# One core, a streaming encoder step: finer norm stages, other kept weights and row buffers; factors begun a tile earlier, kept down weights, a last group of four

## The chip, the cores and the metric

The kernel runs on one core of a Trainium2 chip. The metric is the device time of one execution in microseconds. The kernel before takes 2319.67 us (median of three runs, 2317.66 to 2321.96).

## What is computed

One inference step of an encoder with one layer, in float32, for 2048 prompt rows and 32 sample rows of width 1024:

```python
h = layer_norm(x, ln_in_g, ln_in_b)
z = h @ w_in                                  # 2304 columns: three head groups
o = concat(rg_lru(...), retention(...), sliding_window_attention(...))
h = layer_norm(ALPHA * h + o @ w_out, ln1_g, ln1_b)
f = (silu(h @ w_gate) * (h @ w_up)) @ w_down  # 2816 inner columns
h = layer_norm(ALPHA * h + f, ln2_g, ln2_b)
```

The states of the three groups (convolution rows, recurrent state, retention state, keys and values) are outputs too.

## The kernel before, in words

Each float32 product is made of three products in the fast 32-bit form: an operand is split into a high part (a copy on ScalarE, ACT) and a low part (a subtraction on VectorE, DVE), and high x high, low x high and high x low are added up in PSUM. So each weight tile that TensorE (PE) uses costs a load (issued by SyncE, SP), a copy on ACT (L250 or L1401) and a subtraction on DVE (L254 or L1406), unless the split pair is stored in memory once and loaded back whole.

**First half.** The rows go through six blocks of 256 to 384 rows. For each block there are 18 `W` units (input projection, L908), the three mixers (`mix_a`, `mix_b`, `mix_c`) and 8 `O` units (output projection, L995 to L997), then a layer norm (`ln1`), and the normed rows go to memory twice: as rows, and transposed as columns (`to_memory`: PE transposes into an `sd` bank, ACT copies to one of three `stg` buffers, ACT's queue stores it). Block 0 goes through its gate, up and down products (`G` and `D` units) at the end of this half; `columns0` loads its columns back, `accumulate` (L1024, L1026) adds the down products to the rows. `feed` sets the order of weight loads on SP: up to three staged raw tiles, or a pair kept in memory by an earlier block. `keeps` and `known` say which block stores a pair and which blocks load it: units with odd x are stored by block 1, those with even x by block 2. The side work (norms, mixers, transposes) is written as generators; before each unit `step` lets them go on, one yield at a time, as long as a credit of DVE time lasts. `pipeline` runs the tiles of one stage together; with `apart` set it hands over after each tile's piece. This decides in which order DVE and ACT see the pieces.

**Second half.** The other 1792 rows form two parts of 896. Gate and up products go by f, 22 tiles of 128 inner columns, in `gu`: seven products of 12 matmuls (L1578) with seven left factors (`a11`, `s1`, `s2`, `a12`, `a22`, `s3`, `s4`; sums and differences of quarter matrices, split, made by `columns_first` and `columns_rest` for part 0 and by `columns` for part 1) and seven right factors (`b11`, `t1` and so on, from the weights). Down products go by groups of f in `down` (L1646 to L1648, for 7 row tiles x 2 halves x each f), whose bank `d_add` (L1653) adds to the rows; `GROUPSS` sets the groups, `due` when each comes. Weights are jobs in one list, done ahead in the order of that list by `background` as far as six raw tiles (`ww`) and seven pairs allow. Pairs of the sums `t1` to `t4` are stored in part 0 (`w_keep`) and loaded in part 1 (`w_known`); those of the down weights are made anew in both parts. `ln2` norms finished rows as side work. The last group of part 1 is done in `finale`: five banks are begun with all but the last f, then tile by tile the rest, `stats` (L1711, L1713) and `scales` (L1716, L1717, the power on GpSimd (POOL), L1718) on the tile, and `centre` (L1721), `normal` (ACT, L1726) and `affine` (DVE L1733, POOL L1734) one tile behind.

Row tiles (`tok`) are one pool of 11; PSUM has four `mm` banks, four `sd` banks in the first half, and four `gu` banks from `change()` on, which is called at f = 14 of block 0.

Of the kernel before, what the change touches and what calls it, by code (L numbers as in the profile page):

```python
# [41 lines left out]
GROUPSS = (((0, 3), (3, 6), (6, 9), (9, 12), (12, 15), (15, 17), (17, 19), (19, 22)),) * 2  # L42
# [55 lines left out]
def tile_hybrid_step(ctx: ExitStack, tc: tile.TileContext, io, outs):  # L98
# [190 lines left out]
    def step():  # L289
# [67 lines left out]
    def norm(name, b, g, be):  # L357
# [27 lines left out]
        yield from pipeline([tile_(t, rows) for t, (_, rows) in enumerate(ttiles(b))], 1)  # L385
# [37 lines left out]
    def to_memory(b):  # L423

        def half(t, c0, rows, h):
# [4 lines left out]
            stg = sb.tile([128, 4, 128], F32, name="stg", bufs=3)  # L430
# [33 lines left out]
    def columns0():  # L464
# [3 lines left out]
        for k0, k1 in ((0, 3), (3, 6), (6, 8)):  # L468
            w = row_tile()[:, :(k1 - k0) * n].rearrange("p (k c) -> p k c", c=n)
            sp.dma_start(w, cols0[:, k0:k1, :])  # L470
            yield from wait(4)
# [193 lines left out]
    def mix_b(b):  # L665
# [11 lines left out]
        def chunk(c0, n, state, gi):  # L677
# [56 lines left out]
            yield 0.0  # L734
            pt = sdbank().rearrange("p (f c) -> p f c", f=4)
# [533 lines left out]
    def columns_first():  # L1269

        a = [two(), two()]
# [37 lines left out]

    def columns(s):  # L1310

        for n in ("a11", "s1", "s2", "a12", "a22", "s3", "s4"):
            factor(n)
        ws = []
        for i in range(2):
            k, w = slice(2 * i, 2 * i + 2), {}
            for x, th, kh in (("a", 0, 0), ("d", 0, 1), ("c", 1, 1), ("b", 1, 0)):
                w[x] = row_tile()[:, :2 * HALF].rearrange("p (a b) -> p a b", a=2) if i else two()
                sp.dma_start(w[x], cols1[s, th, kh][:, k, :])
            ws.append((k, w))  # L1320
        for _ in range(5):
            yield 1.2
        while ws:
            k, w = ws.pop(0)

            def hi(n, x):
                act.activation(X[n][1][:, k, :], w[x], AF.Copy)

            def lo(n, x):
                dve.tensor_tensor(X[n][0][:, k, :], w[x], X[n][1][:, k, :].bitcast(F32), op=ALU.subtract)  # L1330

            def sums(x, a, b, op=ALU.subtract):
                dve.tensor_tensor(w[x], w[a], w[b], op=op)  # L1333

            hi("a11", "a")
            hi("a12", "d")
            hi("a22", "c")
            yield 0.1
            lo("a11", "a")
            lo("a22", "c")  # L1340
            yield 2.2
            sums("c", "b", "c", ALU.add)
            hi("s1", "c")
            lo("a12", "d")
            yield 2.2
            sums("b", "a", "b")
            hi("s3", "b")
            sums("a", "c", "a")
            hi("s2", "a")
            yield 2.2  # L1350
            lo("s1", "c")
            sums("d", "d", "a")
            hi("s4", "d")
            yield 2.2
            lo("s3", "b")
            lo("s2", "a")
            yield 2.2
            lo("s4", "d")
            w.clear()
            yield 1.1  # L1360
# [3 lines left out]
    def step_more(more):  # L1364

        owed["more"] = min(owed["more"], 0.0) + 1.3
        while owed["more"] > 0.0:
            c = next(more, None)
            if c is None:
                break  # L1370
# [16 lines left out]

    def new_pair(key):
        at, n = (wp, 3) if clock["made"] % NPAIR < 3 else (sb, NPAIR - 3)
# [4 lines left out]
        if key[0] == 0 and key[2] in ("t1", "t2", "t3", "t4"):  # L1394
# [522 lines left out]
```

## Time and profile before

| | us |
|---|---|
| median of three runs | 2319.67 |
| the profiled execution | 2317.79 |
| its span (first to last instruction) | 2315.8 |
| PE busy | 2243.0 |
| DVE busy | 1479.7 |
| ACT busy | 790.6 |
| granted PE clock, mean | 0.984 |
| data moved | 417.90 MB |

A view of waits says for each pair of lines how long the first engine stood still for the second, how often, and the longest of these. A timeline row has start, length, engine, line, operation, what is written and read, and in brackets the idle time before it with what ended it. SPq and ACTq are the queues that issue transfers.

### The profile page before, as it was taken

Reading aid. Unit: us, or ns where it says so; the run is one execution under the profiler, and the core shown is the slowest. Engines: PE = TensorE matmul, PEld = TensorE weight load, DVE = VectorE, ACT = ScalarE, POOL = GpSimd, SP = SyncE. Lnnn points to the kernel's source line nnn. Section 1 sums busy time; section 2 is a strip of 40 time slices with the busy share of each in tenths; the row PEclk is TensorE's granted clock in tenths of the full one; section 3 lists DMA queues with packets and bytes.
Section 4 is the critical chain, followed back from the end, with each engine's and each line's share of the span. In section 5 each row is a group of like instructions: output and inputs, shape, how many; then the busy total and the mean of one; then the engine's idle time right before and its main releaser. Section 6 shows DMA issues by size and latency. Waiting matters only on the chain.

```text
span 2315.8 us, 31921 instructions
## 1 busy us (share of the span) xinstructions
PE 2243.0 (97%) x12168; PEld 1956.8 (84%) x12168; DVE 1479.7 (64%) x2656; ACT 790.6 (34%) x1585; POOL 158.0 (7%) x236
## 2 busy tenths in 40 slices
PE   8999999999999999989999999999999999999996
PEld 7887888988888879877888988888888888898884
DVE  7795757566446375567876766677787544454557
ACT  5646263351523334234322332322331222232221
POOL 2010201101001011010000000000000000000004
PEclk9999999999999999989999999999999999999998
DMA  6563686767758765764643442433556343343341
GB/s 221 177 197 111 233 268 212 273 225 244 265 184 309 263 199 174 254 210 146 248 158 115 159 151 95 168 127 130 203 187 215 122 154 114 110 154 115 132 132 64
DMA packets 139272, 417.90 MB, mean 180 GB/s; under 512 B 20272, under 2 KB 35440, under 8 KB 127472
## 3 DMA queue, kind: packets, MB, share of 16 engines
q1 hardware_dynamic: 119056, 407.35, 51.4%
q10 hardware_dynamic: 20064, 8.52, 1.3%
q8 instruction: 96, 1.57, 0.3%
q14 instruction: 56, 0.46, 0.1%
HBM read 316.55 MB, written 99.26 MB: 180 GB/s over the span
## 4 chain that ended last, share of the span: by engine, by line
PE 25%; issue 22%; DVE 3%; DMA 1%; POOL 0%; ACT 0%; SPq 0%; DVEq 0%; ACTq 0%; POOLq 0%
PE gu L1578 16%; PE mm L1647 3%; PE mm L1646 3%; PE mm L1648 3%; DVE end_st L1713 0%; DVE tok L1711 0%; DVE end_mv L1721 0%; POOL end_rs L1718 0%; DMA pair<-sum3t 0%; DVE pair L1406 0%; DMA out_y<-tok 0%; DVE xl L1330 0%; DVE tok L1733 0%; DMA tok<-rows 0%; DVE tok L1333 0%
## 5 line engine op out<-in xcount | busy, mean ns | idle before, releaser
L1578 PE MATMUL gu<-xh,pair 128*128 128x448 f32 x2464 | 555.4, 367 | 7.1 <-DVE two L1600 2.9
L1578 PEld LDWEIGHTS gu<-xh,pair 128*128 128x128 f32 x2464 | 463.5, 188 | 50.0 <-issue 3.7
L908 PE MATMUL mm<-hAh,pair 128*128 128x384 f32 (+2 forms) x2432 | 424.6, 323 | 16.4 <-DVE pair L254 5.6
L908 PEld LDWEIGHTS mm<-hAh,pair 128*128 128x128 f32 x2432 | 376.6, 192 | 40.9 <-issue 17.7
L1401 ACT ACTIVATE pair<-ww 128x512 fp32r<-128x512 f32 x308 | 189.8, 626 | 515.8 <-PE mm L1648 237.9
L1578 PE MATMUL gu<-xl,pair 128*128 128x448 f32 x1232 | 303.0, 367 | 0.1
L1406 DVE TENSOR_TENSOR pair<-ww,pair 128x512 fp32r<-128x512 f32 x308 | 208.4, 688 | 147.9 <-ACT pair L1401 137.8
L1578 PEld LDWEIGHTS gu<-xl,pair 128*128 128x128 f32 x1232 | 232.1, 189 | 21.4 <-DVE xl L1330 1.1
L1655 DVE TENSOR_TENSOR tok<-tok,mm 128x512 f32<-128x512 f32 x181 | 124.1, 688 | 161.2 <-PE mm L1648 160.2
L1646 PE MATMUL mm<-pair,g 128*128 128x512 f32 x571 | 225.1, 394 | 1.8 <-DVE tok L1653 1.8
L1647 PE MATMUL mm<-pair,g 128*128 128x512 f32 x571 | 225.1, 394 | 0.0
L1648 PE MATMUL mm<-pair,g 128*128 128x512 f32 x571 | 224.6, 393 | 0.0
L908 PE MATMUL mm<-hAl,pair 128*128 128x384 f32 (+2 forms) x1216 | 211.2, 316 | 0.0
L250 ACT ACTIVATE pair<-stage 128x1024 fp32r<-128x1024 f32 x131 | 138.1, 1055 | 189.1 <-DMA stage<-in_wgu 58.7
L908 PEld LDWEIGHTS mm<-hAl,pair 128*128 128x128 f32 x1216 | 192.5, 192 | 0.0
L254 DVE TENSOR_TENSOR pair<-stage,pair 128x1024 fp32r<-128x1024 f32 x130 | 158.2, 1218 | 31.1 <-ACT pair L250 28.7
L1646 PEld LDWEIGHTS mm<-pair,g 128*128 128x128 f32 x571 | 107.3, 188 | 27.1 <-DVE tok L1653 2.3
L1648 PEld LDWEIGHTS mm<-pair,g 128*128 128x128 f32 x571 | 107.4, 188 | 24.9
L1647 PEld LDWEIGHTS mm<-pair,g 128*128 128x128 f32 x571 | 107.3, 188 | 24.3
L995 PE MATMUL mm<-pair,hCh 128*128 128x512 f32 x216 | 91.1, 422 | 7.3 <-DVE tok L1026 4.7
L997 PE MATMUL mm<-pair,hCh 128*128 128x512 f32 x216 | 86.7, 401 | 0.5 <-DVE pair L254 0.4
L996 PE MATMUL mm<-pair,hCl 128*128 128x512 f32 x216 | 86.9, 402 | 0.2 <-DVE hCl L978 0.2
(297 smaller groups left out, 2641.4 us busy)
## 6 DMA issues: line engine op xcount, KB each, us to landing
pair<-keptW SPq DMA_DIRECT2D x63, 1024.0 KB, 5.4
ww<-in_wgu SPq DMA_DIRECT2D x154, 256.0 KB, 3.2
pair<-keptO SPq DMA_DIRECT2D x28, 1024.0 KB, 4.9
stage<-in_win SPq DMA_DIRECT2D x45, 512.0 KB, 4.7
stage<-in_wgu SPq DMA_DIRECT2D x44, 512.0 KB, 4.2
ww<-in_wdn SPq DMA_DIRECT2D x88, 256.0 KB, 3.1
keptW<-pair SPq DMA_DIRECT2D x36, 512.0 KB, 8.0
stage<-in_wdn SPq DMA_DIRECT2D x22, 512.0 KB, 3.8
```

The lines of the kernel that those rows point to most:

```text
L250: act.activation(whi[u], staged[u], AF.Copy)
L254: eng.tensor_tensor(wlo[u], staged[u], whi[u].bitcast(F32), op=ALU.subtract)
L908: pe.matmul(p, w[:, k, :], a[:, k, :], start=(x == 0 and k == 0), stop=(x == 2 and k == 7))
L995: pe.matmul(o, ah[:, cs], wh[:, x, :], start=first and x == 0, stop=False)
L996: pe.matmul(o, al[:, cs], wh[:, x, :], start=False, stop=False)
L1401: act.activation(pairs[key][1], whole_w[x], AF.Copy)
L1406: dve.tensor_tensor(pairs[key][0], whole_w[x], pairs[key][1].bitcast(F32), op=ALU.subtract)
L1578: pe.matmul(bank[n], w[:, k * 128:k * 128 + 128], a[:, k, :], start=first and x == 0 and k == 0, stop=x == 2 and k == 3, skip_group_check= ...
L1646: pe.matmul(bank, gh, wh, start=first and f == fs[0], stop=False)
L1647: pe.matmul(bank, gl, wh, start=False, stop=False)
L1648: pe.matmul(bank, gh, wl, start=False, stop=last and f == fs[-1])
L1655: dve.tensor_tensor(r, r, bank, op=ALU.add)
```

## The change

In the first half: `keeps` and `known` let units with x divisible by four be stored by block 3 instead of 2, and the last block loads and splits the raw weights for all even x. `step` may give the norm in progress more of the credit, and `norm` hands over after each tile's piece. `to_memory` uses row tiles in place of `stg` for the last block. `columns0` loads one piece ahead. The retention chunk has one more empty turn. `t_unit` takes `gu` banks for the second half of a down group once they exist, and `columns_first` waits six turns.

In the second half: `columns(1)` is started two f earlier and its pieces come in the order in which part 0 is done with the factors; down weight pairs are stored in part 0 and loaded in part 1; part 1's groups end with (15, 18) and (18, 22); the pairs of the last two f and the last inner tile go into buffers of left factors that are no longer needed; `centre` in the finale is two ACT instructions.

```diff
-GROUPSS = (((0, 3), (3, 6), (6, 9), (9, 12), (12, 15), (15, 17), (17, 19), (19, 22)),) * 2
+GROUPSS = (((0, 3), (3, 6), (6, 9), (9, 12), (12, 15), (15, 17), (17, 19), (19, 22)),
+           ((0, 3), (3, 6), (6, 9), (9, 12), (12, 15), (15, 18), (18, 22)))
...
     def keeps(u):
-        return kind in "WO" and b == 1 + (x % 2 == 0)
+        return kind in "WO" and b == 1 + (x % 2 == 0) + (x % 4 == 0)
     def known(u):
-        return kind in "WO" and b > 1 + (x % 2 == 0)
+        if b == NBLK - 1 and x % 2 == 0:
+            return False
+        return kind in "WO" and b > 1 + (x % 2 == 0) + (x % 4 == 0)
...
     def step():
             pace["credit"] -= advance(name)
+        for name in [n for n in pace["turn"] if n in norming]:
+            while name in side and name in norming and pace["credit"] > 0.0:
+                cost = advance(name)
+                pace["credit"] -= cost
+                if cost < 0.5:
+                    break
...
     def norm(name, b, g, be):
-        yield from pipeline([tile_(t, rows) for t, (_, rows) in enumerate(ttiles(b))], 1)
+        yield from pipeline([tile_(t, rows) for t, (_, rows) in enumerate(ttiles(b))], 1, True)
...
     def to_memory(b):
-            stg = sb.tile([128, 4, 128], F32, name="stg", bufs=3)
+            if b < NBLK - 1:
+                stg = sb.tile([128, 4, 128], F32, name="stg", bufs=3)
+            else:
+                if h == 0:
+                    spare[t] = row_tile().rearrange("p (h f c) -> p h f c", h=2, f=4)
+                stg = spare[t][:, h]
...
     def columns0():
+        ahead = load(*ks_[0])
+        yield from wait(6)
+        for i, (k0, k1) in enumerate(ks_):
+            w = ahead
+            ahead = load(*ks_[i + 1]) if i < 2 else None
...
     def t_unit(b, key, kts, wh, wl, wf, first, last):
-            banks[key] = [mmbank() for _ in tiles]
+            banks[key] = [gbank("xzyv"[t], 512) if pg and key == ("D", 1) else mmbank() for t in range(len(tiles))]
...
     def columns_first():
+        yield from wait(6)
...
     def columns(s):
+        def freed(n):
+            while n not in spent:
+                yield 0.0
+        load(0, row_half, "abcd")
         for i in range(2):
+            k = slice(2 * i, 2 * i + 2)
+            yield from freed("a11")
+            hi("a11", "a", k)
+            sums("b", "a", "b")
+            yield 1.1
+            lo("a11", "a", k)
...
     def new_pair(key):
+        store_kept()
+        if outside(key):
+            pair = xp.tile([128, 4, HALF], F32R, name="xlxh"[2 * key[2]:2 * key[2] + 2], bufs=4)
...
-        if key[0] == 0 and key[2] in ("t1", "t2", "t3", "t4"):
+        if key[0] == 0 and key[2] in (0, 1, "t1", "t2", "t3", "t4"):
             kept_pair[key] = pair
...
     def weights_d(s, g, half):
+            if s:
+                if f < f1:
+                    w_known((s, f, half))
+                continue
...
                 w_lo((s, f - 1, half), (s, f - 1, half), True)
+                w_keep((s, f - 1, half))
...
     def gu(s, f, more=None):
+            if s == NPART - 1 and f == FT - 1:
+                t = xp.tile([128, 4, HALF], F32R, name="xl", bufs=4).rearrange("p (a b) c -> p a (b c)", a=2)
+            else:
+                t = xp.tile([128, 2, PART], F32R, name="g", bufs=3)
...
+            if more:
+                if f == FT - 1:
+                    spent.add(left)
+                step_more(more, 1.0)
...
         def centre(t):
-            dve.scalar_tensor_tensor(mv[:, t, 1:2], mv[:, t, 0:1], -1.0, rs[:, t:t + 1],
-                                     op0=ALU.mult, op1=ALU.mult)
+            act.activation(mv[:, t, 1:2], mv[:, t, 0:1], AF.Copy, scale=-1.0)
+            act.activation(mv[:, t, 1:2], mv[:, t, 1:2], AF.Copy, scale=rs[:, t:t + 1])
...
-            gu(s_, f_)
+            if (s_, f_) == (0, FT - 2):
+                more_ = columns(1)
+            gu(s_, f_, more_ if s_ == 0 and f_ >= FT - 2 else None)
```

SP's queue at the start of the last block's input projection: before, every weight (W units x = 0, 1, 2 and on) is a kept pair of 1 MB (`keptW`).

```order
L238 DMA pair<-keptW_2673 128x2048
L238 DMA pair<-keptW_1181 128x2048
L238 DMA pair<-keptW_2762 128x2048
L354 DMA tok<-in_ln_g 128x1024
L354 DMA tok<-in_ln_b 128x1024
L238 DMA pair<-keptW_1293 128x2048
L238 DMA pair<-keptW_2877 128x2048
```

SP at the same place now, the raw tiles being `stage`:

```order
L248 DMA stage<-in_win 128x1024
L241 DMA pair<-keptW_1181 128x2048
L248 DMA stage<-in_win 128x1024
L363 DMA tok<-in_ln_g 128x1024
L363 DMA tok<-in_ln_b 128x1024
L241 DMA pair<-keptW_1293 128x2048
L248 DMA stage<-in_win 128x1024
```

Every second load is a raw tile of 0.5 MB, to be split by ACT and DVE.

DVE in the finale, one tile's turn before (`tok` is a row tile, `end_st`, `end_mv`, `end_rs` its statistics, mean and scale):

```order
L1721 SCALAR_TENSOR_TENSOR end_mv<-end_mv,end_rs 128x1
L1711 TENSOR_TENSOR tok<-tok,mm 128x512
L1713 BN_STATS end_st<-tok 128x6 x2
L1733 TENSOR_TENSOR tok<-tok 128x512
L1711 TENSOR_TENSOR tok<-tok,mm 128x512
L1713 BN_STATS end_st<-tok 128x6 x2
L1716 BN_AGGR end_mv<-end_st 128x2
L1717 TENSOR_SCALAR end_rs<-end_mv 128x1
L1733 TENSOR_TENSOR tok<-tok 128x512
```

DVE in the finale now, one tile's turn:

```order
L1800 TENSOR_TENSOR tok<-tok,mm 128x512
L1802 BN_STATS end_st<-tok 128x6 x2
L1822 TENSOR_TENSOR tok<-tok 128x512
L1800 TENSOR_TENSOR tok<-tok,mm 128x512
L1802 BN_STATS end_st<-tok 128x6 x2
L1805 BN_AGGR end_mv<-end_st 128x2
L1806 TENSOR_SCALAR end_rs<-end_mv 128x1
L1822 TENSOR_TENSOR tok<-tok 128x512
```

The instruction that reads POOL's result is gone from DVE; on ACT two short ones stand ahead of each `normal`.

DVE ahead of block 0's down group of f = 16 and 17, before (`g_t` and `hCl` are the gated inner tile and its low part; `two`, `g`, `xl` belong to `columns_first`):

```order
L965 SCALAR_TENSOR_TENSOR g_t<-g_t,mm 128x288
L254 TENSOR_TENSOR pair<-stage,pair 128x1024
L1296 TENSOR_TENSOR two<-two 128x896
L1297 TENSOR_TENSOR g<-g,two 128x896
L1289 TENSOR_TENSOR xl<-two,xh 128x896
L972 SCALAR_TENSOR_TENSOR g_t<-g_t,mm 128x288
L254 TENSOR_TENSOR pair<-stage,pair 128x1024
L978 TENSOR_TENSOR hCl<-g_t,hCh 128x288
```

DVE at the same place now:

```order
L990 SCALAR_TENSOR_TENSOR g_t<-g_t,mm 128x288
L257 TENSOR_TENSOR pair<-stage,pair 128x1024
L1318 TENSOR_TENSOR g<-two,g 128x896
L997 SCALAR_TENSOR_TENSOR g_t<-g_t,mm 128x288
L257 TENSOR_TENSOR pair<-stage,pair 128x1024
L1003 TENSOR_TENSOR hCl<-g_t,hCh 128x288
```

Three pieces of `columns_first` stood between the two gate operations, now one.

More of the change, by code (lines that the diff above doesn't have):

```diff
@@ L423, in to_memory @@
     def to_memory(b):
+        spare = {}
         def half(t, c0, rows, h):
@@ L467, in columns0, with load @@
         n = ncol(0)
-        for k0, k1 in ((0, 3), (3, 6), (6, 8)):
+        def load(k0, k1):
             w = row_tile()[:, :(k1 - k0) * n].rearrange("p (k c) -> p k c", c=n)
             sp.dma_start(w, cols0[:, k0:k1, :])
-            yield from wait(4)
+            return w
+        ks_ = ((0, 3), (3, 6), (6, 8))
+        ahead = load(*ks_[0])
[3 more added lines that the diff above has]
+            ahead = load(*ks_[i + 1]) if i < 2 else None
             for k in range(k0, k1):
@@ L1308, in columns_rest @@
             yield
+    spent, gone = set(), []
     def columns(s):
-        for n in ("a11", "s1", "s2", "a12", "a22", "s3", "s4"):
-            factor(n)
-        ws = []
-        for i in range(2):
[L1316 to L1340, printed above, removed]
-            yield 2.2
-            sums("c", "b", "c", ALU.add)
-            hi("s1", "c")
-            lo("a12", "d")
-            yield 2.2
[L1346 to L1358, printed above, removed]
+        w = {}
@@ new lines, in load, with row_half, hi @@
+        def load(i, make, names):
+            for x, th, kh in (("a", 0, 0), ("b", 1, 0), ("c", 1, 1), ("d", 0, 1)):
+                if x in names:
+                    w[x] = make()
+                    sp.dma_start(w[x], cols1[s, th, kh][:, 2 * i:2 * i + 2, :])
+        def row_half():
+            return row_tile()[:, :2 * HALF].rearrange("p (a b) -> p a b", a=2)
+        def hi(n, x, k):
+            if k.start == 0:
+                factor(n)
+            act.activation(X[n][1][:, k, :], w[x], AF.Copy)
@@ L1359, in columns, with step_more @@
             w.clear()
+            if i == 0:
+                load(1, two, "abcd")
+                for _ in range(3):
+                    yield 1.3
             yield 1.1
     owed = {"more": 0.0}
-    def step_more(more):
-        owed["more"] = min(owed["more"], 0.0) + 1.3
+    def step_more(more, rate=1.5):
+        owed["more"] = min(owed["more"], 0.0) + rate
         while owed["more"] > 0.0:
             c = next(more, None)
-            if c is None:
+            if not c:
                 break
@@ L1386, in tile_hybrid_step, with outside, store_kept @@
     kept_pair = {}
-    def new_pair(key):
+    def outside(key):
+        return key[0] == NPART - 1 and key[1] >= FT - 2 and key[2] in (0, 1)
+    stores = []
+    def store_kept():
+        for d, x in stores:
+            sp.dma_start(d, x)
+        stores.clear()
+    def new_pair(key):
+        store_kept()
+        if outside(key):
+            pair = xp.tile([128, 4, HALF], F32R, name="xlxh"[2 * key[2]:2 * key[2] + 2], bufs=4)
+            pair = pair.rearrange("p a b -> p (a b)")[:, :1024].rearrange("p (a b) -> p a b", a=2)
+            pairs[key] = pair[:, 0, :], pair[:, 1, :]
+            return pair
         at, n = (wp, 3) if clock["made"] % NPAIR < 3 else (sb, NPAIR - 3)
@@ L1423, in fn @@
         def fn():
-            sums[key[1:]] = dr.tile([128, 2, 512], F32, name="sum%d%s" % key[1:])
-            sp.dma_start(sums[key[1:]], kept_pair[key].bitcast(F32))
+            d = sums[key[1:]] = dr.tile([128, 2, 512], F32, name="sum%d%s" % key[1:])
+            stores.append((d, kept_pair[key].bitcast(F32)))
+        ends[key] = len(jobs)
         jobs.append(("store", fn, ()))
@@ L1432, in w_known @@
         ends[key] = len(jobs)
-        jobs.append(("pair", fn, ()))
+        jobs.append(("last" if outside(key) else "pair", fn, ()))
     def free(x):
@@ L1501, in job @@
         kind, fn, _ = jobs[clock["done"]]
-        if kind == "pair" and clock["pairs"] == NPAIR:
+        if kind == "pair" and clock["pairs"] == NPAIR or kind == "last" and len(gone) < 3:
             return False
@@ L1510, in background @@
         clock["slot"] += 1
+        store_kept()
         loads()
@@ L1565, in catch_up, with gu @@
                 f()
-    def gu(s, f):
+    def gu(s, f, more=None):
         bank, v = {}, {}
@@ L1635, in gu @@
             step()
+            if s == NPART - 1 and f == FT - 1 and left in ("a11", "s1", "s2"):
+                del X[left]
+                gone.append(left)
+            if more:
+                if f == FT - 1:
+                    spent.add(left)
+                step_more(more, 1.0)
             if left == "s2":
@@ L1801, in tile_hybrid_step @@
         if s_ < NPART - 1:
-            more_ = columns(s_ + 1)
             for g_ in ending(s_):
```

35 lines of the change are left out of this document (34 added, 1 removed).

## The prediction

> **What bounds the kernel now.** I read the page's busy times first, then the chain of waits of the matrix engine (PE), then the timeline around each long wait.
>
> ```profile
> ## 1 busy us (share of the span) xinstructions
> PE 2243.0 (97%) x12168; PEld 1956.8 (84%) x12168; DVE 1479.7 (64%) x2656; ACT 790.6 (34%) x1585; POOL 158.0 (7%) x236
> ```
>
> PE is busy for 2243.0 of 2315.8 us. No matmul is removed, so all there is to win lies in PE's idle 73 us, 16.6 of them after the last matmul (2298.80 + 0.42, quoted below), and in the slow clock that follows an idle stretch. PE's waits in the whole span (us in total, times, longest):
>
> ```profile
> PE mm L1704 <- DVE tok L1711: 6.6, 4, 2.7
> PE mm L908 <- DVE pair L254: 5.6, 5, 2.3
> PE mm L908 <- ACT pair L250: 4.9, 1, 4.9
> PE mm L995 <- DVE tok L1026: 4.7, 1, 4.7
> PE sd L813 <- ACT stg L431: 3.5, 2, 2.2
> ...
> PE gu L1578 <- DVE two L1600: 2.9, 1, 2.9
> PE mm L908 <- DMA pair<-keptW: 2.8, 2, 1.7
> ...
> PE mm L995 <- ACT hCh L973: 2.7, 1, 2.7
> ...
> PE gu L1578 <- ACT two L1586: 2.2, 1, 2.2
> PE mm L908 <- ACT hAh L473: 2.1, 1, 2.1
> PE gu L1578 <- ACT xh L1327: 2.0, 1, 2.0
> ...
> PE sd L737 <- DVE b_o L731: 1.7, 2, 1.5
> ```
>
> They are single events at stage borders, each with another cause. The finale shows what one costs beside its length (PE's timeline: start, length, then the idle time before it):
>
> ```profile
> 2260.37 0.39 PE L1704 MATMUL mm<-pair,g 128*128 128x512 f32 x1
> ...
> 2278.87 0.39 PE L1706 MATMUL mm<-pair,g 128*128 128x512 f32 x1
> 2281.21 0.67 PE L1704 MATMUL mm<-pair,g 128*128 128x512 f32 x1 [1.95 <-DVE tok L1711]
> ...
> 2284.66 0.46 PE L1706 MATMUL mm<-pair,g 128*128 128x512 f32 x1
> ...
> 2298.80 0.42 PE L1706 MATMUL mm<-pair,g 128*128 128x256 f32 x1
> ```
>
> From 2260.37 to 2278.87 stand 81 matmuls without a wait, so one step is 18.50/80 = 0.231 us. After the wait of 1.95 us eight steps take 2284.66 - 2281.21 = 3.45 us where 8 x 0.231 = 1.85 would do: a **cold price** of 1.6 us on top of the wait. I charge it to each removed wait of about 2 us or more. The Trainium skill (TensorE: Matmul & The Clock Gate, "What's actually happening") says that PE falls to half rate after at least one idle window of about 3.4 us. By that only the waits of 4.9 and 4.7 us would carry a cold price; the row after 1.95 us disagrees, and the row decides here.
>
> **The change part by part.** Sums are made against the profiled execution: 2317.8 us with a span of 2315.8, 1.9 below the median of 2319.7.
>
> *Last group of four and the finale.* Engines there are tied as follows (DVE, then POOL, then ACT):
>
> ```profile
> 2268.23 0.69 DVE L1711 TENSOR_TENSOR tok<-tok,mm 128x512 f32<-128x512 f32 x1 [2.90 <-PE mm L1706]
> ...
> 2272.24 0.16 DVE L1721 SCALAR_TENSOR_TENSOR end_mv<-end_mv,end_rs 128x1 f32<-128x1 f32 x1 [0.66 <-POOL end_rs L1718]
> ...
> 2276.12 0.15 DVE L1717 TENSOR_SCALAR end_rs<-end_mv 128x1 f32<-128x1 f32 x1
> ...
> 2277.32 1.24 DVE L1721 SCALAR_TENSOR_TENSOR end_mv<-end_mv,end_rs 128x1 f32<-128x1 f32 x1 [0.44 <-POOL end_rs L1718]
> ...
> 2282.28 0.15 DVE L1717 TENSOR_SCALAR end_rs<-end_mv 128x1 f32<-128x1 f32 x1
> ...
> 2306.98 0.15 DVE L1717 TENSOR_SCALAR end_rs<-end_mv 128x1 f32<-128x1 f32 x1
> ```
> ```profile
> 2276.36 0.93 POOL L1718 TENSOR_TENSOR end_rs<-end_rs,mhalf 128x1 f32<-128x1 f32 x1 [0.59 <-DVE end_rs L1717]
> 2277.25 1.29 POOL L1734 TENSOR_TENSOR tok<-tok 128x512 f32<-128x512 f32 x1
> ```
> ```profile
> 2278.59 1.24 ACT L1726 ACTIVATE tok<-tok,end_mv,end_rs 128x1024 f32<-128x1024 f32 x1 [4.92 <-DVE end_mv L1721]
> ```
>
> DVE's period is 2282.28 - 2276.12 = 6.16 us a tile, against 18 x 0.231 = 4.2 of PE: DVE is the bound, and of its period 0.44 + 1.24 = 1.68 is `centre`, which waits for POOL's power and then sits until POOL's add ends (2277.25 + 1.29 = 2278.54). Before the finale PE now does one f less: 14 x 3 = 42 matmuls, 9.7 us, move from a stretch that PE bounds into one that DVE bounds. There DVE's first bank comes at 45 x 0.231 + 0.7 = 11.1 us instead of 2268.23 - 2260.37 = 7.9. With `centre` on ACT the period is 6.16 - 1.68 = 4.5 if DVE waits for nothing; but the first half's product needs `normal`, which comes 0.1 + 0.9 (power) + 0.3 (two short activations, estimated from the 0.16 of the same work on DVE) + 1.24 = 2.6 us after the scales, and DVE has only 2.0 us of work before it, so 5.2. PE needs 24 x 0.231 = 5.5 a tile, but leads by the five banks filled early. DVE ends its last scales at 11.1 + 3.2 (first tile) + 6 x 5.2 = 45.5 after the finale's start; before it was 2306.98 + 0.15 - 2260.37 = 46.8. So -9.7 - 1.3 = **-11.0**; with a period of 6.16 it is -5.2, with 4.5 it is -15.
>
> The tail behind those scales I leave as it is: `whole` takes the place of `centre` right when POOL's add starts, as `centre` did in the row of 1.24. The Trainium skill (SBUF — State Buffer, "Who interferes with whom") says that a DVE instruction with two SBUF inputs and a GpSimd one that reads SBUF exclude each other for the whole instruction, and the row of 0.16 with POOL idle agrees; without that lock the tail would be 1.1 us shorter.
>
> *Row buffers for the last block's columns.* The one wait of 4.9 us comes from here:
>
> ```profile
> 993.78 0.60 ACT L431 ACTIVATE stg<-sd 128x512 f32<-128x512 f32 x1 [4.85 <-DMA cols<-stg]
> ```
>
> The fourth copy waits for the first of three `stg` buffers to be stored, and the weight split L250 is queued behind it on ACT. With two row tiles for four copies nothing waits: 4.9 + 1.6 = **-6.5**. If the row tiles come free late, half of it stays: -3.
>
> *Norm stages, `columns0` loaded ahead.* Block 0's columns come late since their load stands behind four weight loads on SP, and L254 comes late behind long norm pieces on DVE:
>
> ```profile
> 801.55 12.62 SPq L245 DMA_DIRECT2D stage<-in_wgu  x4
> 814.21 0.43 SPq L470 DMA_DIRECT2D tok<-cols  x1
> ```
> ```profile
> 834.77 2.47 DVE L382 SCALAR_TENSOR_TENSOR tok<-tok,ln_rs 128x1024 f32<-128x1024 f32 x2
> ```
> ```profile
> 839.99 1.51 PE L908 MATMUL mm<-hAh,pair 128*128 128x288 f32 x8 [1.97 <-DVE pair L254]
> ```
>
> The last load of columns now stands ahead of those four (order of SP), so 2.1 + 1.6 go; norm pieces come singly, so 2.0 + 1.6 can go. Together 7.3; I take **-6**, bounds 0 and -8 (DVE's total work is the same, only its grain changes).
>
> *Kept weights.* Columns of these rows: stretch, PE, PEld, DVE, ACT, POOL, clock, share of the DMA engines, GB/s.
>
> ```profile
> 250.00:300.00 50.00, 49.82 (x310) 46.90 (x308) 33.52 (x73) 14.05 (x30) 10.90 (x13) 1.00 0.88 311
> 400.00:450.00 50.00, 49.86 (x307) 47.19 (x306) 29.06 (x72) 11.97 (x34) 7.81 (x16) 1.00 0.85 300
> 700.00:750.00 50.00, 46.73 (x376) 43.69 (x375) 33.16 (x79) 18.11 (x57) 6.52 (x16) 0.97 0.89 318
> ```
> ```profile
> 299.57 1.06 ACT L250 ACTIVATE pair<-stage 128x1024 fp32r<-128x1024 f32 x1 [4.81 <-DMA stage<-in_win]
> ```
>
> The memory is near its most where blocks 2, 3 and 5 begin. The waits for `keptW` (2.8 + 1.6) are in block 5, where nine W units now bring 0.5 MB instead of 1; the waits for `stg` (3.5 + 1.6) are in block 2, where ACT stands 4.81 us behind a late load; five W units there lose their 1 MB of stores. 9.5 in all, I take -7.5. Block 3 gets 0.5 MB more for each of five units, at 300 GB/s already: +2, between 0 and the 5.1 that block 2 pays. The nine splits added in block 5 go to DVE, which is busy 33 of 50 us. Net **-5.5**, bounds +2 and -9.5.
>
> *Smaller edits.* One more empty turn ahead of the transposes of `b_o`: **-1.5** of 1.7. `columns_first` starts six turns later; on DVE one piece of it is left ahead of the last gate of its group instead of three, so of 2.7 + 1.6 I take **-3** (bounds 0 and -4.3). `gu` banks for the second half of the early down groups: PE no longer waits 4.7 + 1.6 for L1026, but the next unit's L254 stands behind the same L1026 and L1022 on DVE, and `gu` must wait for its bank at the border: **-1.5** (+1 to -6).
>
> *Left factors in the last tile.* Part 1's factors are begun inside part 0's last f, so the wait for L1327 (2.0 + 1.6) goes. DVE is busy there for 39.70 of 50 us (third number of the row):
>
> ```profile
> 1650.00:1700.00 50.00, 47.97 (x212) 40.03 (x210) 39.70 (x52) 19.82 (x28) 0.00 (x0) 0.98 0.47 159
> ```
>
> It gets about 7 us more in an f of 7 x 12 matmuls, so **-2.2**, bounds +3 and -3.6.
>
> *Kept down weights.* 44 stores of 512 KB in part 0, 44 loads of 512 instead of 256 KB in part 1, 44 splits less on ACT and DVE. PE waited for none of the splits, so no gain; the stores are hidden behind seven pair buffers. **0**, at worst +4 if the longer loads hold up row loads on SP.
>
> The waits for L1600 and L1586 (2.9, 2.2) follow six row loads that stand in the same place of SP's queue: unchanged. **Sum:** -11.0 - 6.5 - 6 - 5.5 - 1.5 - 3 - 1.5 - 2.2 = -37.2; 2317.8 - 37.2 = 2280.6, and 1.9 higher for a median: **2282.5 us**.
>
> **The rivals.** *The waits move* (0.20): in the first half every engine's order is shuffled, and the same DVE and DMA lateness meets PE elsewhere. For it: the waits have many causes. Against it: DMA bytes do fall in blocks 2 and 5. Only the finale and the row buffers stay: 17.5 us, 2302.
>
> *Slower* (0.07): the 44 new stores on SP. Each waits for DVE's split and stands ahead of the next raw weight loads; if each costs PE 1.0 us, 44 - 37.2 leaves 2326.5. It decides from 37.2/44 = 0.85 us a store. Against it: no row of the waits names a raw weight (`ww`) load though the `sum` stores are in that queue already.
>
> *No cold price for short waits* (0.03): the clock rule above as a mechanism here: the half clock after 1.95 us came by chance. Then about six of the 1.6 us are not won, weighted by what I took some 7.5: 2290.
>
> *Eaten up* (0.05): the finale gives 5 and new DMA waits in block 3 and DVE waits at the border of the parts take that and the rest: 2319.
>
> **How the numbers follow.** The forecast has 0.65. About 0.2% (4.6 us) is what a measurement of this kernel can tell from no change. Faster: 0.65 + 0.20 + 0.03 = 0.88; same 0.05; slower 0.07. The range goes from all best bounds, 2319.7 - 15 - 6.5 - 8 - 9.5 - 1.7 - 4.3 - 6 - 3.6 = 2265, over the moved waits to 2306.
>
> **What would show it.** Right: no DVE `centre` and a period near 5.2 us in the finale; no wait of ACT for `cols<-stg` near 990; no PE wait for `keptW`; PE's waits below 30 us in all. Wrong: PE waits for `ww` or `sum` loads, or new waits of 2 us at blocks 3 and 5 or in part 0's last f.

## The result and the profile after

The changed kernel takes 2297.86 us (median of four runs, 2295.39 to 2301.05), beside 2320.82 for the kernel before on the same chip (2317.66 to 2322.71). The ratio is 0.9903, with a 95% interval of 0.9885 to 0.9922: 23 us faster, 37.2 forecast. The profiled execution took 2299.39 with a span of 2297.6, so 18.2 less than the span of before.

The busy times, and the waits of PE (us in total, times, longest):

```profile
PE 2236.0 (97%) x12171; PEld 1950.3 (85%) x12171; DVE 1456.6 (63%) x2611; ACT 789.9 (34%) x1575; POOL 173.2 (8%) x236
```
```profile
PE sd L722 <- DVE b_k L715: 7.0, 2, 5.5
PE mm L933 <- DVE pair L257: 5.1, 9, 1.1
PE gu L1022 <- DVE pair L257: 4.9, 2, 4.5
PE gu L1656 <- DVE two L1678: 2.7, 1, 2.7
...
PE gu L1656 <- ACT two L1664: 2.6, 1, 2.6
...
PE mm L933 <- DMA pair<-keptW: 2.1, 1, 2.1
...
PE mm L1736 <- DVE g L1704: 1.8, 1, 1.8
...
PE sd L838 <- ACT c_pt L874: 1.6, 1, 1.6
```

The finale's waits (before: 6.6) are gone from the list, and so is the 4.9 us behind `cols<-stg`. Two rows have grown: the one for `c_pt`, of which there was a single wait of 0.3, and the one for `b_k`. Before it was

```profile
PE sd L698 <- DVE b_k L691: 2.6, 2, 1.5
```

The wait for `keptW` is still there.

**Finale.** First bank, two scales one tile apart and the last scales on DVE; then ACT's second `centre` instruction and `normal`:

```profile
2255.66 0.69 DVE L1800 TENSOR_TENSOR tok<-tok,mm 128x512 f32<-128x512 f32 x1 [6.94 <-PE mm L1795]
...
2279.30 0.15 DVE L1806 TENSOR_SCALAR end_rs<-end_mv 128x1 f32<-128x1 f32 x1
...
2284.51 0.15 DVE L1806 TENSOR_SCALAR end_rs<-end_mv 128x1 f32<-128x1 f32 x1
...
2287.30 0.69 DVE L1822 TENSOR_TENSOR tok<-tok 128x512 f32<-128x512 f32 x1 [0.66 <-ACT tok L1815]
...
2289.90 0.15 DVE L1806 TENSOR_SCALAR end_rs<-end_mv 128x1 f32<-128x1 f32 x1
...
2291.28 1.44 DVE L1829 SCALAR_TENSOR_TENSOR tok<-tok,end_rs 128x384 f32<-128x384 f32 x1
```
```profile
2285.70 0.29 ACT L1811 ACTIVATE end_mv<-end_mv,end_rs 128x1 f32<-128x1 f32 x1 [0.80 <-POOL end_rs L1807]
2286.03 1.24 ACT L1815 ACTIVATE tok<-tok,end_mv,end_rs 128x1024 f32<-128x1024 f32 x1
```
```profile
2244.31 0.39 PE L1793 MATMUL mm<-pair,g 128*128 128x512 f32 x1
```

The period is 2284.51 - 2279.30 = 5.21 us and the last scales come 2289.90 + 0.15 - 2244.31 = 45.7 after the finale's start, with 5.2 and 45.5 forecast. As forecast, the period is that of a chain: DVE's scales, POOL's power, three instructions on ACT, and DVE, which waits 0.66 us for `normal`. The finale's start itself is 2260.37 - 2244.31 = 16.1 us earlier; 10 of that arise after the first f of part 1, since 42 matmuls less stand ahead of the finale (9.7 forecast).

**A new wait near 122.** DVE, then PE:

```profile
110.13 4.75 DVE L407 TENSOR_TENSOR tok<-tok 128x1024 f32<-128x1024 f32 x4
...
115.83 2.34 DVE L407 TENSOR_TENSOR tok<-tok 128x1024 f32<-128x1024 f32 x2
...
121.54 0.41 DVE L715 TENSOR_TENSOR b_k<-sd,tb 32x256 f32<-32x256 f32 x1
```
```profile
122.00 0.42 PE L722 MATMUL sd<-zb 64*32 64x32 f32 x4 [5.48 <-DVE b_k L715]
122.35 5.38 PE L933 MATMUL mm<-hAh,pair 128*128 128x384 f32 x16
```

L407 is `gained`, which applies the input norm's weights to block 0. It counts as a norm, so `step`'s new loop spends what credit is left on it: four pieces on end, then two. Before, single pieces of 1.2 us stood there, with other work between them:

```profile
112.82 1.22 DVE L398 TENSOR_TENSOR tok<-tok 128x1024 f32<-128x1024 f32 x1
...
114.96 1.22 DVE L398 TENSOR_TENSOR tok<-tok 128x1024 f32<-128x1024 f32 x1
```

`b_k` and, behind it, half of the next chunk's key-query products on PE wait for them. The 16 matmuls after the wait take 5.38 us, 0.336 each, at half clock.

**A new group of waits near 735**, in the last block (ACT, PE, and SP's queue):

```profile
735.84 1.06 ACT L253 ACTIVATE pair<-stage 128x1024 fp32r<-128x1024 f32 x1 [5.29 <-DMA stage<-in_win]
```
```profile
734.39 1.56 PE L933 MATMUL mm<-hAh,pair 128*128 128x256 f32 x8 [2.05 <-DMA pair<-keptW]
...
737.43 1.64 PE L838 MATMUL sd<-kb,zq 64*128 64x192 f32 x4 [0.63 <-ACT stg L447]
740.69 1.65 PE L838 MATMUL sd<-kb,zq 64*128 64x192 f32 x4 [1.62 <-ACT c_pt L874]
```
```profile
724.99 1.68 SPq L473 DMA_DIRECT2D rows<-tok  x3
726.77 1.14 SPq L241 DMA_DIRECT2D pair<-keptW  x1
727.96 1.21 SPq L248 DMA_DIRECT2D stage<-in_win  x1
```

ACT stands 5.29 us before the split of a raw weight, and `stg` and `c_pt` of the attention are queued behind it. The granted clock is half from 735.04 to 745.28.

**Two shorter ones.** ACT and PE near 990, and DVE and PE at the end of block 0's down products:

```profile
991.29 0.60 ACT L447 ACTIVATE tok<-sd 128x512 f32<-128x512 f32 x1 [0.81 <-ACT tok L447]
...
992.81 1.06 ACT L253 ACTIVATE pair<-stage 128x1024 fp32r<-128x1024 f32 x1 [0.92 <-ACT tok L447]
```
```profile
993.92 1.32 PE L933 MATMUL mm<-hAh,pair 128*128 128x288 f32 x8 [1.72 <-ACT pair L253]
...
1081.73 0.79 PE L1022 MATMUL gu<-pair,hCh 128*128 128x512 f32 x1 [4.50 <-DVE pair L257]
```
```profile
1077.61 1.28 DVE L1051 TENSOR_TENSOR tok<-tok,mm 128x512 f32<-128x512 f32 x2
1078.81 1.73 DVE L1047 TENSOR_TENSOR tok<-tok,mm 32x256 f32<-32x256 f32 x4
1080.47 1.21 DVE L257 TENSOR_TENSOR pair<-stage,pair 128x1024 fp32r<-128x1024 f32 x1
```

No copy waits for a store any more, but PE still waits 1.72 for the split behind them. And the wait that the `gu` banks removed stands at 1081 now, behind the same adds, as the prediction had said it could.

### The profile page after: what moved, and what is told of

The parts are those of the page before. It is cut to its first block, busy times and chain, and to the rows that moved or that the text cites. A ratio compares the mean times of both kernels' runs of the same rounds, so it can differ in the third digit from the quotient of the medians.

```text
span 2297.6 us, 31930 instructions
## 1 busy us (share of the span) xinstructions
PE 2236.0 (97%) x12171; PEld 1950.3 (85%) x12171; DVE 1456.6 (63%) x2611; ACT 789.9 (34%) x1575; POOL 173.2 (8%) x236
## 5 line engine op out<-in xcount | busy, mean ns | idle before, releaser
L933 PE MATMUL mm<-hAh,pair 128*128 128x384 f32 (+2 forms) x2432 | 423.6, 322 | 10.2 <-DVE pair L257 5.1
L933 PEld LDWEIGHTS mm<-hAh,pair 128*128 128x128 f32 x2432 | 373.9, 191 | 36.0 <-issue 18.7
L1472 ACT ACTIVATE pair<-ww 128x512 fp32r<-128x512 f32 x264 | 162.1, 625 | 466.3 <-PE mm L1737 233.7
L1477 DVE TENSOR_TENSOR pair<-ww,pair 128x512 fp32r<-128x512 f32 x264 | 178.6, 688 | 133.2 <-ACT pair L1472 130.4
L253 ACT ACTIVATE pair<-stage 128x1024 fp32r<-128x1024 f32 x151 | 159.4, 1057 | 240.4 <-DMA stage<-in_win 67.7
L1735 PE MATMUL mm<-pair,g 128*128 128x512 f32 x557 | 219.8, 395 | 2.9 <-DVE tok L1742 2.4
L1736 PE MATMUL mm<-pair,g 128*128 128x512 f32 x557 | 219.8, 395 | 1.8 <-DVE g L1704 1.8
L1737 PE MATMUL mm<-pair,g 128*128 128x512 f32 x557 | 219.2, 394 | 0.0
L257 DVE TENSOR_TENSOR pair<-stage,pair 128x1024 fp32r<-128x1024 f32 x150 | 183.4, 1222 | 43.8 <-ACT pair L253 43.8
L1744 DVE TENSOR_TENSOR tok<-tok,mm 128x512 f32<-128x512 f32 x167 | 114.2, 687 | 151.6 <-PE mm L1737 151.3
L933 PE MATMUL mm<-hAl,pair 128*128 128x384 f32 (+2 forms) x1216 | 209.1, 314 | 0.0
L933 PEld LDWEIGHTS mm<-hAl,pair 128*128 128x128 f32 x1216 | 190.3, 190 | 0.0
L1735 PEld LDWEIGHTS mm<-pair,g 128*128 128x128 f32 x557 | 104.7, 188 | 28.8 <-DVE tok L1742 3.7
L1736 PEld LDWEIGHTS mm<-pair,g 128*128 128x128 f32 x557 | 104.7, 188 | 25.8 <-DVE g L1704 2.1
L1737 PEld LDWEIGHTS mm<-pair,g 128*128 128x128 f32 x557 | 104.7, 188 | 24.3
L1687 ACT ACTIVATE two<-two 128x448 f32<-128x448 f32 x44 | 25.5, 579 | 176.5 <-DVE two L1685 176.5
L1020 PE MATMUL mm<-pair,hCh 128*128 128x512 f32 x196 | 81.0, 413 | 0.1
L1022 PE MATMUL mm<-pair,hCh 128*128 128x512 f32 x196 | 77.4, 395 | 1.0 <-DVE pair L257 1.0
```

Source lines behind the costliest of these rows:

```text
L253: act.activation(whi[u], staged[u], AF.Copy)
L257: eng.tensor_tensor(wlo[u], staged[u], whi[u].bitcast(F32), op=ALU.subtract)
L933: pe.matmul(p, w[:, k, :], a[:, k, :], start=(x == 0 and k == 0), stop=(x == 2 and k == 7))
L1020: pe.matmul(o, ah[:, cs], wh[:, x, :], start=first and x == 0, stop=False)
L1022: pe.matmul(o, ah[:, cs], wl[:, x, :], start=False, stop=last and x == 1)
L1472: act.activation(pairs[key][1], whole_w[x], AF.Copy)
```

## The experiments

Theory: the second half pays what was forecast, and in the first half two edits bring new waits of their own, near 122 (credit for `gained`) and near 735 (raw weights in the last block), some 8 and 10 us. Rivals: DVE's and ACT's lateness has a common cause and moves with any edit; or the terms were too large in many places. Each kernel is the changed one with the edit shown. A ratio's interval is about 0.0017 to each side, so two ratios within 0.0025 (6 us) are not told apart; a single stage is read finer from the starts of PE's products there. Two executions of the same instructions differ too: where gate products begin, the changed kernel's profile has 1087.0, and two kernels that differ from it only later 1083.2 and 1083.5. Where a stage of the first half is given in us below, it is read from the starts of the same products of the input projection and of the gates (L908 before, L933 in the changed kernel).

**Gain pieces out of the credit loop.**

```diff
-        for name in [n for n in pace["turn"] if n in norming]:
+        for name in [n for n in pace["turn"] if n in norming and n != "g0"]:
```


> The changed kernel, with block 0's gain pieces (the name g0) taken out of the new loop that gives a turn's remaining credit to norm pieces. Theory (the bursts of four gain pieces make block 1's b_k late): the wait of PE for b_k of 5.48 us near 122 and the half clock behind it go, some 8 us, so about 2291 for the span-like time of 2299. Rival (the same DVE work comes late somewhere else in that block): within 2 us of the changed kernel.

Measured: 2291.36 us, ratio 0.9887 (0.9874 to 0.9901), span 2289.4.

```profile
PE sd L722 <- DVE b_k L715: 3.7, 2, 2.3
```

The longest wait falls from 5.5 to 2.3 and block 1's next product starts 5.1 us earlier (117.3 for 122.4). Up to 166 us nothing of it is given back. By the ratios alone (0.0016 apart) the two kernels are not told apart, but the place repeats: this wait is 5.48 or 5.49 in all eight kernels here that spend credit on gain pieces, and 2.28 in all five that do not. So the theory holds for 3.2 us of the wait.

The other 2.28 us have a cause of their own, which is not the credit: before, PE did not stand there at all. The kernel with the norm stages of before (below) has this wait too, though DVE's order up to `b_k` is there that of before. What differs on PE is that the transposes of `b_o` come a turn later, between the next chunk's transposes and its key-query products. By the code they then hold one of the four `sd` banks, so half of these products must wait until `b_k` has read the bank of the chunk's transposes. This points at the extra empty turn of the retention chunk; no run takes that turn alone.

**No credit loop at all.**

```diff
-        for name in [n for n in pace["turn"] if n in norming]:
-            while name in side and name in norming and pace["credit"] > 0.0:
...
```


> The changed kernel without the new loop in the step function: remaining credit is no longer given to any norm pieces. Theory (the loop costs 8 us in block 0 and saves the waits of the blocks behind, some 3 to 5 us near 820 and 840): 3 to 5 us faster than the changed kernel, near 2295, and 3 to 5 us behind the kernel without the gain pieces in the loop. Rival (the loop is worth nothing elsewhere, and the earlier load of columns and the single norm pieces did the rest): 8 us faster, as fast as the kernel without the gain pieces in the loop.

Measured: 2314.88 us, ratio 0.9989 (0.9981 to 0.9998). Both expectations failed, by 20 us and more: without the loop nearly the whole change is lost.

```profile
PE sd L411 <- DVE tok L385: 20.3, 3, 8.6
```

The rows are not normed when the next block's transposes (L411) need them, three times. By the code, `norm` hands over after each piece now, so it takes more turns, and without extra credit it is late. The finer stages and the loop are one edit: beside the kernel above, the loop is worth 0.9989 - 0.9887 = 0.0102, some 24 us.

**Kept pairs in the whole last block.**

```diff
-        if b == NBLK - 1 and x % 2 == 0:
-            return False
```


> The changed kernel, with the last block's even units of W and O loaded as kept pairs again, not as raw weights that are split. Theory (the raw loads stand behind row stores and arrive late, so that ACT waits 5.29 us for a stage and PE stands in three places near 735): the new waits of about 10 us near 735 go and before's waits for kept pairs (4.4 us) may come back, so 5 to 10 us faster, 2290 to 2295. Rival (the row stores of the norm make everything behind them late, in whichever form the weights come): within 2 us of the changed kernel.

Measured: 2287.29 us, ratio 0.9869 (0.9855 to 0.9882). Stretch, PE, PEld, DVE, ACT, POOL, clock, share of DMA engines and GB/s of that place, for the changed kernel and this one:

```profile
720.00:750.00 30.00, 25.70 (x174) 22.47 (x174) 15.86 (x35) 15.88 (x48) 1.65 (x7) 0.83 0.59 208
```
```profile
720.00:750.00 30.00, 28.21 (x232) 25.06 (x230) 14.30 (x35) 16.20 (x53) 1.28 (x7) 1.00 0.92 326
```

With 326 GB/s instead of 208 PE does more, at full clock. From 734 to 764 the kernel gains 9.1 us on the changed one. Fewer bytes were no help there. By the ratios it is 8 us faster than the changed kernel, as the theory had it; its median lies 3 below the theory's range.

**The same number of raw units, in one piece.** Is it the raw weights, or that raw and kept ones alternate? By `feed`, a pair's load after a raw unit is issued only once that unit is split.

```diff
-        if b == NBLK - 1 and x % 2 == 0:
+        if b == NBLK - 1 and (x >= 9 if kind == "W" else x % 2 == 0):
```


> The changed kernel with as many raw W units in the last block, but in one piece: the first nine W units come as kept pairs, the last nine raw, instead of one about the other. The new waits near 735 lie at the tenth unit, so the raw units stand at that place still. Theory (one about the other, a pair's load is issued only after the raw unit ahead of it is split, so loads go out two at a time and late): no wait of ACT for a stage above 2 us and no wait of PE for a pair near 735, 8 to 12 us faster, a span of 2286 to 2290, as with kept pairs in the whole block. Rival (a raw weight's split on ACT stands ahead of the attention's copies, however its load is issued): the waits stay at that place, within 3 us of the changed kernel.

Measured: 2293.46 us, ratio 0.9900 (0.9881 to 0.9918); the theory of alternation falls. ACT, in this kernel:

```profile
729.28 1.06 ACT L253 ACTIVATE pair<-stage 128x1024 fp32r<-128x1024 f32 x1 [6.15 <-DMA stage<-in_win]
```

The first raw unit waits 6.15 us. From 727.7 to 747.7 PE does what the kernel with kept pairs does from 729.2 to 739.0, 10 us more, and the clock is at half for 13.65 us of it. What both have in common is a raw split on ACT, ahead of the attention's pieces, for a load that lands late. Why it lands late (row stores and 1 MB pairs ahead of it on SP, or the issue itself) was argued from SP's rows, not tried.

**Choice of kept weights of before.**

```diff
-        return kind in "WO" and b == 1 + (x % 2 == 0) + (x % 4 == 0)
+        return kind in "WO" and b == 1 + (x % 2 == 0)
-        if b == NBLK - 1 and x % 2 == 0:
-            return False
-        return kind in "WO" and b > 1 + (x % 2 == 0) + (x % 4 == 0)
+        return kind in "WO" and b > 1 + (x % 2 == 0)
```


> The changed kernel with the choice of kept weights of before in every block: every odd unit kept from block 1, every even one from block 2, no exception in the last block. It differs from the kernel with the last block's kept pairs only in each fourth unit, stored one block earlier. Theory of the prediction (stores are what makes loads late where block 2 begins): the wait for stg near 305 returns, 3.5 and 1.6 us, block 3 saves up to 2, so some 3 us behind the kernel with the last block's kept pairs, a span near 2287. Rival (the waits there hang on the order on ACT and DVE, not on bytes): within 1.5 us of it, a span near 2284.

Measured: 2295.85 us, ratio 0.9897 (0.9881 to 0.9912).

```profile
PE sd L836 <- ACT stg L445: 4.0, 2, 2.2
```

The wait for `stg` of before is back, and at 310 us this kernel falls 6.6 behind the one with kept pairs in the last block. So storing each fourth unit a block later is worth some 6.5 us (3 expected), and the raw weights of the last block cost some 8 (0.9903 - 0.9869): together the edit of the kept weights gives nothing.

**Norm stages of before.**

```diff
-        for name in [n for n in pace["turn"] if n in norming]:
...
-        yield from pipeline([tile_(t, rows) for t, (_, rows) in enumerate(ttiles(b))], 1, True)
+        yield from pipeline([tile_(t, rows) for t, (_, rows) in enumerate(ttiles(b))], 1)
```


> The changed kernel with the norm stages of before: the tiles' pieces are issued together in one turn again, and no remaining credit goes to norms; the columns are still loaded ahead. Theory of the prediction (long norm pieces make a weight split late): block 0's new 8 us go, of the two waits near 820 and 840 the one for the columns (3.7) stays away and the one for the split (3.6) returns, so a span near 2293. Rival (the finer pieces are worth nothing in themselves, the credit only pays for the turns that they take): a span near 2289, as with the gain pieces left out.

Measured: 2298.79 us, ratio 0.9908 (0.9892 to 0.9924), as the changed kernel.

```profile
PE mm L927 <- DVE pair L257: 8.8, 8, 2.6
```

It gains 4.7 near 122, loses 3.0 near 43, where a wait for a split of 2.6 is back, 2.8 near 521 and 1.9 near 843. The finer stages thus bring about 5 (0.9908 - 0.9887, within the interval's reach) where the gain pieces are left out, and about nothing with them. The theory's 2293 was missed by the median, met by the profiled span (2293.0).

**Three `stg` buffers in the last block.**

```diff
-            if b < NBLK - 1:
+            if b < NBLK:
```


> The changed kernel with the three stg buffers for the last block's columns too, no row tiles. Theory of the prediction: the wait of 4.9 us near 990 and 1.6 us of slow clock return, a span 6.5 us longer, near 2304. Rival (other work is late there by now, as the waits of 1.9 and 0.8 us near 996 in the changed kernel show): 3 to 5 us longer, 2301 to 2302. Second rival (the changed blocks ahead of it have moved the stores): no wait, within 1 us of the changed kernel.

Measured: 2303.14 us, ratio 0.9929 (0.9916 to 0.9943), by the ratios 6 us slower than the changed kernel, just told apart; from 988 to 1004 us PE loses 5.0.

```profile
995.78 0.60 ACT L447 ACTIVATE stg<-sd 128x512 f32<-128x512 f32 x1 [4.85 <-DMA cols<-stg]
```

The wait returns with the same 4.85. The row buffers are worth what was forecast for them.

**`centre` on DVE.**

```diff
-            act.activation(mv[:, t, 1:2], mv[:, t, 0:1], AF.Copy, scale=-1.0)
-            act.activation(mv[:, t, 1:2], mv[:, t, 1:2], AF.Copy, scale=rs[:, t:t + 1])
+            dve.scalar_tensor_tensor(mv[:, t, 1:2], mv[:, t, 0:1], -1.0, rs[:, t:t + 1],
+                                     op0=ALU.mult, op1=ALU.mult)
```


> The changed kernel with the finale's centre on DVE again, as one operation behind the power. Theory of the prediction (DVE sets the finale, 5.2 us a tile with centre on ACT and 6.16 with it on DVE): the period is 6.1 to 6.2 us, the end 5.8 us later, near 2305. Rival (PE or ACT sets the finale by now): the period stays within 0.3 us of 5.2 and the time within 2 us.

Measured: 2301.46 us, ratio 0.9931 (0.9917 to 0.9944).

```profile
2278.74 0.15 DVE L1806 TENSOR_SCALAR end_rs<-end_mv 128x1 f32<-128x1 f32 x1
2279.93 1.22 DVE L1810 SCALAR_TENSOR_TENSOR end_mv<-end_mv,end_rs 128x1 f32<-128x1 f32 x1 [0.44 <-POOL end_rs L1807]
...
2284.86 0.15 DVE L1806 TENSOR_SCALAR end_rs<-end_mv 128x1 f32<-128x1 f32 x1
```

Period 6.12; from f = 4 of part 1 to the end it loses 5.3 us on the changed kernel, 5.8 forecast. The chain through DVE sets the finale, not PE's work.

**Down weights of part 1 raw again** (but for the last group).

```diff
-            if s:
-                if f < f1:
-                    w_known((s, f, half))
-                continue
+            if f < f1 and s and f >= FT - 4:
+                w_known((s, f, half))
+                continue
+            if s and f1 == FT:
+                continue
...
-                w_keep((s, f - 1, half))
+                if not s and f - 1 >= FT - 4:
+                    w_keep((s, f - 1, half))
```


> The changed kernel with the down weights of part 1 loaded raw and split again, as before, but for the last group of four, which stays kept; 36 stores fewer in part 0. Theory of the prediction (all of that lies beside PE's work): within 1.5 us of the changed kernel. Rival (the stores and the longer loads cost 4 us in part 0 and 1): 4 us faster, near 2294. Second rival (the splits of part 1 stand between the column pieces and the tanh work on DVE and ACT at the border of the parts): 2 to 4 us slower.

Measured: 2297.19 us, ratio 0.9911 (0.9894 to 0.9929). No difference that can be told, as forecast: the 36 stores that this kernel leaves out, of 44, had cost nothing that can be seen.

**Common banks for the second half of the early down groups.**

```diff
-            banks[key] = [gbank("xzyv"[t], 512) if pg and key == ("D", 1) else mmbank() for t in range(len(tiles))]
+            banks[key] = [mmbank() for t in range(len(tiles))]
```


> The changed kernel with the second half of the early down groups in the common banks again, not in those of gu. Theory of the prediction (the wait of PE for tok near 1035, 4.7 and 1.6 us, comes back, and the wait that took its place near 1082 goes): 1.5 us slower, between 1 us faster and 6 us slower. Rival (the wait is only moved along the row, DVE is late there whatever the banks): within 1 us of the changed kernel.

Measured: 2296.43 us, ratio 0.9911 (0.9893 to 0.993).

```profile
PE mm L1020 <- DVE tok L1051: 3.2, 1, 3.2
```

The old wait is back, with 3.2, and the one of 4.5 at 1081 is gone. The wait is moved; the ratios differ by 0.0008, some 2 us, which is not told apart from nothing.

**Both repairs together.** Gain pieces out of the loop, kept pairs in the last block.

> The changed kernel with two edits together: block 0's gain pieces left out of the new credit loop, and the last block's even units loaded as kept pairs again. Theory (two separate new waits, near 122 and near 735): the gains add, 8 and 11 us by the traces of the single edits, so a span near 2277 and a median near 2279. Rival (the engines' lateness has one common cause, and what is won first is waited for later): no better than the kept pairs alone, a span near 2284.

Measured: 2283.18 us, ratio 0.9837 (0.9816 to 0.9858), span 2281.9. It is faster than the kept pairs alone by 0.0032, some 7 us, so the gains add in the medians (one of five runs took 2275.68). The expected span of 2277 was missed by 5, that of the rival (2284) by 2: in the profiled run what the gain pieces bring is 4.8 at 823 us, and 2.2 of it are left near the end.

**And row loads one a turn.** The two waits that the prediction left unchanged were put down to six row loads on SP. In the kernel of the two repairs DVE waits there:

```profile
1106.36 0.69 DVE L1483 TENSOR_TENSOR ww<-ww 128x512 f32<-128x512 f32 x1 [4.17 <-DMA ww<-in_wgu]
```
```diff
         for _ in range(min(ahead, len(more))):
             load_rows(after, (more.pop(0),))
+            yield from wait(1)
```


> The kernel with both single edits (gain pieces out of the credit loop, kept pairs in the whole last block), and one more: the second norm's six row loads at the start of the gated products go out one a turn, not all six at once ahead of the next weights. In the kernel without it DVE waits 4.17 us for a weight that stands behind them, and PE waits 2.7 and 2.3 us near 1109 and 1120. Theory (the six loads on SP make the weights late, as the prediction had it for these two waits): DVE's wait and both waits of PE go, with 1.7 us of slow clock, some 5 to 7 us faster than without it, a span near 2276. Rival (DVE's own work of the second norm makes the gates late): one of the two waits stays, within 2 us.

Measured: 2276.59 us, ratio 0.9814 (0.9797 to 0.983): the fastest of all, 42 us under before.

```profile
PE mm L1734 <- DVE tok L1741: 2.5, 1, 2.5
...
PE gu L1655 <- ACT two L1663: 0.3, 1, 0.3
```

One wait of PE is gone and 0.3 is left of the other; gate products of f = 3 start 6.3 us earlier, counted from f = 0. 4.2 of that are lost near 1750, where a down wait of 2.5 is new; by the ratios (0.0023 apart) the edit is worth 5 us, a little less than can be told. What shows the theory is that the two waits go.

## Why the prediction came out as it did

The direction was right and 2297.86 lies in the range, but 15.4 us above the forecast: the sum was 37.2, the medians give 23. Term by term:

| term | forecast | measured |
|---|---|---|
| finale and last group | -11.0 | -11 and 1.1 in the tail (trace) |
| row buffers | -6.5 | -6 (three `stg`) |
| columns ahead (-3.7), norm stages (the rest) | -6 | -3.9 (trace) and about 0 |
| kept weights | -5.5 | about 0: -6.5 and +8 |
| `columns_first` | -3 | -4.2 at that place (trace) |
| left factors in the last tile | -2.2 | -1.3 (trace) |
| extra turn for `b_o` | -1.5 | waits for `b_o` -1.2 without the gain bursts; a wait for `b_k` of 2.28 (cause argued) |
| `gu` banks | -1.5 | 0 to -2 |
| kept down weights | 0 | 0 |
| waits for `two` | 0 | 0 |

- **Right in mechanism and size:** the finale (a chain through DVE as its bound, 5.2 us a tile, 42 matmuls moved), the row buffers, the columns loaded ahead (the wait of 2.15 near 819 and its half clock are gone, and that place gains 3.9 us in each of the thirteen changed kernels; 3.7 forecast), the down weights, the two unchanged waits and their cause. In the tail `whole` did not take the place of `centre`: its first operation needs only the mean and runs while POOL still does the power, which saves 1.1. Its second one sits through POOL's add (1.44 us for 384 columns), which agrees with the rule that was cited (the Trainium skill, SBUF — State Buffer, "Who interferes with whom").
- **Failed: "DVE's total work is the same, only its grain changes"** (norm stages, bounds 0 and -8). The grain of `gained` became coarser, not finer: the loop's condition takes in the name `g0`. It was to be seen in DVE's order, four L407 on end and then two. Beside the kernel without these bursts that costs 5 to 6 us (trace; 3.7 by the ratios), and eats what the finer norms bring. I also charged the loop no worth of its own, which the run without it corrects by 24 us: single pieces without credit are late.
- **Not in the sum: what the extra turn delays.** The prediction gave the turn only the wait for `b_o` that it shortens. Between 111 and 125 us PE loses 2.9 to 4.3 us on before in the five kernels without the gain bursts, where the wait of 2.28 stands, and 1.6 come back with `b_o`. So this term was likely a loss, but no run shows it alone.
- **Failed: "the waits for `keptW` are in block 5, where nine W units now bring 0.5 MB instead of 1".** The step from bytes to waits was wrong there. A kept pair needs no engine, while a raw unit puts a split on ACT ahead of the attention's pieces; its load was late by 5.29 us and PE stood three times. The same reasoning was right at block 2, where stores went (6.5 gained, 5.1 forecast).
- **Undersized: the cold price of 1.6 us.** It came from one wait of 1.95. With the wait of 5.48, and with three waits within 7 us, the clock was at half for 10.24 us; PE worked 5.4 and 8.0 us of that at half speed, which costs 2.7 and 4.0. But one profile does not fix such a price: in the thirteen changed kernels PE works between 3.1 and 6.3 us at half clock after the wait near 120 us, which costs 1.6 to 3.1, and the largest price stands behind a wait of 2.28, not of 5.48. So 1.6 is the low end. It was undersized for removed waits too: behind the wait for `hCh` of 2.65 in the kernel before, the clock was at half for 6.83 us, which fits what that place gained beyond the forecast.
- **The rivals.** "The waits move" gave 2302, nearer to the result than the forecast. Its count came near, but its reason held only in part: the wait at the `gu` banks did move, while the new waits near 735 and, but for 2.28 us, near 122 come from single edits and go with them, and with both repaired the kernel takes 2283.18, near the forecast of 2282.5. "Slower" by the stores did not happen. "No cold price" had a point, since short waits are often not followed by half clock (last section), but on the whole the price was too low, not too high. PE's waits sum to 46 us, where below 30 was to show the forecast right; that sign, the waits for `keptW`, and a new wait of 1.8 in part 0's last f showed the forecast of the gain too high.

## What to carry to other kernels

When a scheduler's rule names a class of work, look up in the order of instructions who else is in that class. Loading a prepared operand is worth more than halving its bytes, if the raw one puts a step on an in-order engine that others wait on: price the queue behind that step, not the transfer. A finer grain needs the turns to run in; test grain and credit apart.

## What was not expected of the hardware

Two waits of nearly the same length, 12 us apart, on PE in the changed kernel:

```profile
1124.21 3.33 PE L1656 MATMUL gu<-xh,pair 128*128 128x448 f32 x8 [2.69 <-DVE two L1678]
...
1135.87 1.91 PE L1656 MATMUL gu<-xh,pair 128*128 128x448 f32 x8 [2.57 <-ACT two L1664]
```

The eight matmuls after the first take 3.33 us, after the second 1.91. In all traces here the granted clock falls to half for 3.41 us or a multiple of it (6.83, 10.24, 13.65), but for the stretch behind the last matmul, with which the record ends. In the changed kernel waits of PE of 1.72 us near 994, of 1.82 in part 0's last f and of 2.6 near 1136 left no half clock; one of 2.05 near 734, one of 2.7 near 1124, and two of 1.15 and 1.51 within 3 us near 229, did. The single wait's length alone does not decide it, and repeats show it best: the wait of 1.81 to 1.83 us in part 0's last f stands in all thirteen changed kernels, and half clock goes with it in seven of them, none in six. Nor does the length set how long it lasts: one of 5.48 and three that sum to 4.30 went with 10.24 us each here, but in six other kernels the same wait of 5.48 went with 6.83. The Trainium skill (TensorE: Matmul & The Clock Gate, "What's actually happening") asks for an idle window of about 3.4 us before the rate falls; the length of the slow stretch agrees with that figure, the length of idle time before it does not.
